# A decoder trunk whose first FFN multiplies tokens that are not yet normed, and loads x and its first weights in alternating halves

## The chip, the cores and the metric

The kernel runs on one core of a Trainium2 chip. The metric is the device time of one execution in microseconds; runs are told by their median. The engines of the core are TensorE (PE; its weight loads are shown as PEld), VectorE (DVE), ScalarE (ACT), GpSimd (POOL) and SyncE (SP), which issues most transfers.

## The reference, cut to what matters

Two layers of a hybrid decoder trunk work on 256 tokens of width 1024 in float32. The change lies in the first FFN of the first layer alone.

```python
def rms_norm(x, w):
    x32 = x.astype(jnp.float32)
    y = x32 * lax.rsqrt(jnp.mean(x32 * x32, axis=-1, keepdims=True) + EPS)
    return (y * w.astype(jnp.float32)).astype(x.dtype)

def swiglu(h, w_gate, w_up, w_down):
    return (jax.nn.silu(h @ w_gate) * (h @ w_up)) @ w_down

for l in range(DEPTH):                                   # DEPTH = 2
    x = x + 0.5 * swiglu(rms_norm(x, ffn1_norm[l]), ffn1_w_gate[l], ffn1_w_up[l], ffn1_w_down[l])
    x = x + hybrid_mixer(rms_norm(x, mix_norm[l]), ...)  # two head groups, HGRN2 and FoX
    x = x + memory_cross_attention(rms_norm(x, cross_norm[l]), rms_norm(mem, mem_norm[l]), ...)
    x = x + 0.5 * swiglu(rms_norm(x, ffn2_norm[l]), ffn2_w_gate[l], ffn2_w_up[l], ffn2_w_down[l])
return rms_norm(x, final_norm)
```

The width of an FFN (D_FF) is 2816. The norm of a token is a gain per feature times one number per token, the mean square to the power -1/2. The text calls this number the token's power.

## The kernel before, in words

**Products in three parts.** Every float32 operand is split in a high part in a reduced format (the cast writes it) and a low part (the operand minus its high part). A product is three TensorE instructions: high by high, high by low, low by high (`mm3`, L439 to L441). ScalarE makes the high parts (`whi` of weights, `xfh` of tokens), VectorE the low ones (`wlo`, `xfl`). For the first FFN of the first layer the gain per feature is multiplied into the weights while they are split (`split_k`, L147 and L148): it stands on the partitions of the weight tiles, in the column `g0`, which TensorE makes from a loaded row by a transpose (L229) and VectorE copies (L230).

**Weights.** All weights are one list of pieces of at most 1 MB (`plan`), four row blocks of 128 rows by 512 columns for the gate and the up matrices. `fetch` issues the loads on SP's queue into three buffers (`rawp`), `split` makes the two parts in seven buffers of two row blocks each (`wp`). A piece is fetched two pieces ahead of the one that is split and split one ahead of the one that is used. `split_block` splits one row block of a piece.

**Tokens.** x is resident as `xs`, two token blocks of 128 partitions by 1024 features. For the products, 128x128 squares are transposed on TensorE into a PSUM tile of four (`pt`), and `put_split` makes the two parts from it (ScalarE, then VectorE, L366 and L367).

**An FFN.** The 2816 columns are taken in five chunks of 512 and one of 256. The first chunk keeps tokens on the output's partitions: gate and up products of 512 columns with the tokens as stationary operand. For the others (`wstat`) weights are stationary, the 256 tokens are the columns, and a PSUM bank holds two column blocks of 128 features; `use_g` and `use_u` evict it: Silu on ScalarE (L697), multiplication on VectorE (L706), and a split. The down product `rows_to_residual` goes over all 22 row blocks, and its result times 0.5 is added to `xs` on VectorE (L628), after which the next norm begins.

**The beginning.** The first FFN's first gate block is written out by hand in `first_chunk`. Within an `in_order` block each engine keeps the order of the text; elsewhere the framework places an instruction in its engine's queue by a simulated time and by priority. Before that, `warm_up` issues transposes of the identity into a bank that nobody reads. `norm(t)` takes the squares of half 0 on ScalarE (L488) and of half 1 on VectorE (L489), sums them (L340) and lets GpSimd raise the sum to the power -1/2 (L341); `scaled` multiplies a half of x by it on VectorE (L494); `turn` transposes four squares (L501); `put` splits them. The first token block's products with weight blocks 0 to 3 come first, then 12 more warm-up transposes, then the second token block's norm and transposes, and the rest of the 16 products of the block (48 instructions).

**The rest.** The kernel's main line and side tasks (constants, the two head groups, the memory) are generators; `drive` picks by a clock of estimated times what is written next. The estimates (`yield` of a time) of the first chunk are the same in both kernels.

Of the kernel before, what the change touches and what calls it, by code (L numbers as in the profile page):

```python
# [8 lines left out]
F32 = mybir.dt.float32  # L9
# [4 lines left out]
ALU = mybir.AluOpType  # L14
# [31 lines left out]
def hymba_kernel(  # L46
# [82 lines left out]
    def fetch(i):  # L129
        while len(raws) <= min(i, len(plan) - 1):  # L130
            src, nk, cw, _ = plan[len(raws)]
            r = rawp.tile([P, 4 * 520], F32, name=nm("raw"), tag="raw")
            rv = r[:, :nk * cw].rearrange("p (k c) -> p k c", k=nk)
            n = (4, 2)[len(raws)] if len(raws) < 2 else 1
            for k0 in range(0, nk, nk // n):
                nc.sync.dma_start(out=rv[:, k0:k0 + nk // n, :], in_=src[:, k0:k0 + nk // n, :])
            raws.append(r)

    def split_k(i, sl, k, hi, lo):

# [66 lines left out]

    grow = cp.tile([8, P], F32, name="grow")
    nc.scalar.dma_start(out=grow, in_=ffn1_norm[0].rearrange("(k p) -> k p", p=P))
    for t in range(NT):  # L210
        for j in range(2):
            sl = slice(j * 512, (j + 1) * 512)
            nc.sync.dma_start(out=xs[:, t, sl], in_=x_d[0, t * P:(t + 1) * P, sl])
        fetch(t)


    ident = cp.tile([P, P], F32, name="ident")
# [3 lines left out]
    def warm_up(n):  # L221
        for i in range(n):
            nc.tensor.transpose(warm[:, (i % 4) * P:(i % 4 + 1) * P], ident, ident)
# [1 line left out]
    g0 = cp.tile([P, 8], F32, name="g0")  # L225
    g0t = smp("g0t")
    with in_order():
        warm_up(14)
        nc.tensor.transpose(g0t[:, 0:8], grow, ident[0:8, 0:8])  # L229
        nc.vector.tensor_copy(out=g0, in_=g0t[:, 0:8])  # L230
        gcols["first"] = g0
        warm_up(12)
    neghalf = cp.tile([P, 4], F32, name="neghalf")
    nc.vector.memset(neghalf, -0.5)

# [242 lines left out]

    def first_chunk(f, psa_, psb_):

        psa_ += [acc(), acc()]
        rs = [small(1, "rs") for _ in range(NT)]
        hn = [s4([P, D], F32, "hn") for _ in range(NT)]

        def norm(t):
            ss = small(2, "ss")
            x = xs[:, t, :]
            nc.scalar.activation(hn[t][:, 0:512], half(x, 0), AF.Square, scale=1.0 / 32.0, accum_out=ss[:, 0:1])  # L488
            nc.vector.tensor_tensor_reduce(out=hn[t][:, 512:1024], in0=half(x, 1), in1=half(x, 1), scale=1.0 / 1024.0,  # L489
                                           scalar=0.0, op0=ALU.mult, op1=ALU.add, accum_out=ss[:, 1:2])  # L490
            inv_rms(ss, rs[t])

        def scaled(t, j):
            nc.vector.tensor_scalar(out=half(hn[t], j), in0=half(xs[:, t, :], j), scalar1=rs[t], scalar2=None,  # L494
                                    op0=ALU.mult)

        def turn(t, b):
            pt = smp("pt")
            for j in range(4):
                kt = 4 * b + j  # L500
                nc.tensor.transpose(pt[:, j * P:(j + 1) * P], hn[t][:, kt * P:(kt + 1) * P], ident)  # L501
            return pt

        def put(pt, t, b):
            sl = slice(t * P, (t + 1) * P)
            put_split(f.h[b][:, :, sl], f.l[b][:, :, sl], pt.rearrange("p (k t) -> p k t", k=4))

        with in_order():
            norm(0)
            for j in range(2):  # L510
                scaled(0, j)
            p0 = [turn(0, b) for b in range(2)]
            pa = split_block(0, 0)
            put(p0[0], 0, 0)
            for kt in range(4):
                if kt:
                    pa += split_block(0, kt)
                xmm(psa_, f, kt, 0, pa[kt], 512)
            warm_up(12)
            put(p0[1], 0, 1)  # L520
            norm(1)
            pa += split_block(1, 0)
            for j in range(2):
                scaled(1, j)
            p1 = [turn(1, b) for b in range(2)]
            pa += split_block(1, 1)
            for b in range(2):
                put(p1[b], 1, b)
            for kt in (4, 5):
                xmm(psa_, f, kt, 0, pa[kt], 512)  # L530
            for kt in range(6):
                xmm(psa_, f, kt, 1, pa[kt], 512)
            for kt in (6, 7):
                pa += split_block(1, kt - 4)
                for t in range(NT):
                    xmm(psa_, f, kt, t, pa[kt], 512)
            taken[0] = 2
        yield 16 * T512
        yield from xstat(f, 512, psb_)

    def wstat(f, use, cw=512):

# [69 lines left out]
    def rows_to_residual(act, n, scale, tail, nxt, need=None):  # L612
        ps = [[[(acc(), 0, 512)] for _ in range(2)] for _ in range(NT)]
        if nxt.last:
            ps[1][1] = [(ps[1][1][0][0], 0, 256), (smp(), 256, 256)]
        head = n - tail

        def one(i, t, h, pc, pieces_):
            hi, lo = act(i, t)
            for a, c, w in pieces_:  # L620
                sl = slice(h * 512 + c, h * 512 + c + w)
                mm3(a[:, 0:w], hi, lo, pc[0][:, sl], pc[1][:, sl], i == 0, i == n - 1)

        def resid(t, h, piece):
            a, c, w = piece
            sl = xs[:, t, h * 512 + c:h * 512 + c + w]
            with tc.high_priority(offset=HP):
                nc.vector.scalar_tensor_tensor(out=sl, in0=a[:, 0:w], scalar=scale, in1=sl, op0=ALU.mult, op1=ALU.add)  # L628

        for i in range(0, head, 2):  # L630
            pc = take()
            for j in range(2):
                if need is not None:
                    yield need(i + j)
                for t in range(NT):
                    for h in range(2):
                        one(i + j, t, h, pc[j], ps[t][h])
                yield 4 * T512
        pcs = []
        for i in range(head, n, 2):  # L640
            pcs += take()
        for t in range(NT):
            for h in range(2):
                for piece in ps[t][h]:
                    for i in range(head, n):
                        if need is not None:
                            yield need(i)
                        one(i, t, h, pcs[i - head], [piece])
                        yield T512 * piece[2] / 512
                    resid(t, h, piece)  # L650
            nxt.start(t)


    def ffn(cur, nxt_w, last=False, first=False):
# [4 lines left out]
        def h_task(c, hs, cw):  # L659
# [25 lines left out]
        for ci, (c0, cw) in enumerate(FCH):  # L685
            g, u = [], []
            if ci == 0:
                if first:
                    yield from first_chunk(f, g, u)
                else:  # L690
                    yield from xstat_first(f, cur.ev, g, u)
                mult(ci, silu(g, cw), u, cw)
            else:
                s_ = s4([P, NT, 512], F32, "sil")

                def use_g(b, ps):
                    nc.scalar.activation(s_[:, b], ps, AF.Silu)  # L697

                yield from wstat(f, use_g, cw)
                hi = s4([P, 4, S], F32R, "hth")  # L700
                lo = s4([P, 4, S], F32R, "htl")
                hts[ci] = (hi, lo)

                def use_u(b, ps):
                    h = s_[:, b]
                    nc.vector.tensor_tensor(out=h, in0=h, in1=ps, op=ALU.mult)  # L706
# [237 lines left out]
    def mixer(cur, l, consts, nxt_w):  # L944
# [74 lines left out]
        def act(kt, t):  # L1019
            return oT.hi(kt, t), oT.lo(kt, t)  # L1020

        yield from rows_to_residual(act, KT, 1.0, TAIL, nxt, lambda kt: ev_h if kt < 4 else ev_p[kt - 4])
        return nxt, kc, vc, mf

    def memory_task(mf, ev):
# [32 lines left out]
    def cross(cur, kc, vc, mf, nxt_w):  # L1058
# [56 lines left out]
        def act(kt, t):  # L1115
            return oT.hi(kt, t), oT.lo(kt, t)

        yield from rows_to_residual(act, KT, 1.0, TAIL, nxt, lambda kt: evs[kt // 2])
        return nxt


# [45 lines left out]
```

## Time and profile before

| | |
|---|---|
| median of 3 runs | 1242.22 us (1242.09 to 1242.61) |
| the profiled execution | 1242.66 us, its span 1240.8 us |
| TensorE busy | 1227.8 us, 99% of the span |
| VectorE busy | 767.1 us, 62% |
| ScalarE busy | 653.6 us, 53% |
| loads | 219.72 MB, mean 177 GB/s |

The profile is one execution. Its page gives busy times by engine, the span in 40 slices, the chain of work that ended last, and groups of instructions by line. L439 is line 439 of the kernel; `acc<-xfh,whi` names the output tile and the input tiles. The span's start is 0 in all times of the order of instructions. The mean granted clock of TensorE was 0.999 of full speed. TensorE's instructions are pipelined: the duration of one is longer than the distance between the starts of two.

### The profile page before, as it was taken

The numbers are of one execution on the slowest core, as the hardware profiler recorded it, in microseconds if no ns is written. First come the engines' busy times: TensorE is split into PE (matmuls) and PEld (weight loads), VectorE is DVE, ScalarE is ACT, GpSimd is POOL, SyncE is SP. The second block draws the span as 40 slices with busy tenths as digits, with TensorE's granted clock in tenths as the row PEclk, the third lists the DMA queues.
The fourth block names the chain that finished last, engine by engine and source line by source line (L and its number), as shares of the span: only waits on it lengthen the run. The fifth ranks groups of instructions, "written<-read, shape, count | busy, mean of one in ns | idle before, by whom it ended". The sixth has DMA issues, their size and how long they took to land.

```text
span 1240.8 us, 21619 instructions
## 1 busy us (share of the span) xinstructions
PE 1227.8 (99%) x9074; PEld 1122.9 (90%) x9074; DVE 767.1 (62%) x1180; ACT 653.6 (53%) x1022; POOL 36.9 (3%) x52
## 2 busy tenths in 40 slices
PE   9999999999999999999999999999999999999997
PEld 7999888999989889998889998889998898999986
DVE  7756546588866674464474554475887766545643
ACT  7555535568854454353354454366786555444532
POOL 0000000011000000000000000000010000000000
PEclk9999999999999999999999999999999999999999
DMA  8555654643544374565474556465444533555640
GB/s 320 170 191 171 237 191 152 221 135 139 170 153 170 102 254 141 199 206 202 136 255 137 204 181 220 142 216 193 144 147 170 187 131 109 190 184 170 238 170 35
DMA packets 100258, 219.72 MB, mean 177 GB/s; under 512 B 4128, under 2 KB 16704, under 8 KB 100160
## 3 DMA queue, kind: packets, MB, share of 16 engines
q1 hardware_dynamic: 100000, 218.07, 51.7%
q8 instruction: 71, 1.16, 0.4%
q10 hardware_dynamic: 160, 0.27, 0.1%
q14 instruction: 27, 0.22, 0.1%
HBM read 217.28 MB, written 1.05 MB: 176 GB/s over the span
## 4 chain that ended last, share of the span: by engine, by line
PE 93%; DVE 3%; ACT 1%; POOL 1%; issue 1%; DMA 0%; POOLq 0%; SPq 0%; DVEq 0%; ACTq 0%
PE acc L439 29%; PE acc L440 29%; PE acc L441 29%; PE pt L360 1%; DVE wlo L144 1%; PE al L739 1%; DVE wlo L148 1%; ACT whi L147 0%; POOL rs L341 0%; POOL hrs L808 0%; PE cpo L440 0%; DVE pp L867 0%; PE cs L440 0%; PE cs L439 0%; PE cs L441 0%
## 5 line engine op out<-in xcount | busy, mean ns | idle before, releaser
L144 DVE TENSOR_TENSOR wlo<-raw,whi 128x1024 fp32r<-128x1024 f32 (+1 forms) x324 | 389.1, 1223 | 275.4 <-ACT whi L143 274.4
L143 ACT CAST whi<-raw 128x1024 fp32r<-128x1024 f32 (+1 forms) x324 | 330.4, 1048 | 276.1 <-PE acc L441 137.1
L439 PE MATMUL acc<-xfh,whi 128*128 128x256 f32 x1536 | 432.7, 282 | 0.0
L440 PE MATMUL acc<-xfl,whi 128*128 128x256 f32 x1536 | 431.6, 281 | 0.2
L441 PE MATMUL acc<-xfh,wlo 128*128 128x256 f32 x1536 | 430.1, 280 | 0.0
L440 PEld LDWEIGHTS acc<-xfl,whi 128*128 128x128 f32 x1536 | 290.3, 189 | 0.9 <-DVE xfl L367 0.7
L439 PEld LDWEIGHTS acc<-xfh,whi 128*128 128x128 f32 x1536 | 289.0, 188 | 0.8
L441 PEld LDWEIGHTS acc<-xfh,wlo 128*128 128x128 f32 x1536 | 289.7, 189 | 0.0
L439 PE MATMUL acc<-whi,hth 128*128 128x512 f32 (+1 forms) x352 | 136.4, 388 | 0.0
L440 PE MATMUL acc<-wlo,hth 128*128 128x512 f32 (+1 forms) x352 | 136.3, 387 | 0.0
L441 PE MATMUL acc<-whi,htl 128*128 128x512 f32 (+1 forms) x352 | 135.8, 386 | 0.0
L439 PE MATMUL acc<-whi,xfh 128*128 128x512 f32 (+1 forms) x256 | 94.8, 370 | 0.6 <-ACT xfh L366 0.6
L440 PE MATMUL acc<-wlo,xfh 128*128 128x512 f32 (+1 forms) x256 | 94.0, 367 | 0.0
L441 PE MATMUL acc<-whi,xfl 128*128 128x512 f32 (+1 forms) x256 | 93.6, 366 | 0.1
L441 PEld LDWEIGHTS acc<-whi,htl 128*128 128x128 f32 x352 | 66.2, 188 | 14.5
L439 PEld LDWEIGHTS acc<-whi,hth 128*128 128x128 f32 x352 | 66.1, 188 | 14.4
L440 PEld LDWEIGHTS acc<-wlo,hth 128*128 128x128 f32 x352 | 66.1, 188 | 14.0
L148 DVE SCALAR_TENSOR_TENSOR wlo<-raw,g,whi 128x512 fp32r<-128x512 f32 (+1 forms) x96 | 61.9, 703 | 26.0 <-PE acc L441 18.5
L147 ACT ACTIVATE whi<-raw,g 128x512 fp32r<-128x512 f32 (+1 forms) x96 | 58.2, 678 | 24.8 <-PE acc L440 18.0
L439 PEld LDWEIGHTS acc<-whi,xfh 128*128 128x128 f32 x256 | 48.1, 188 | 9.2 <-ACT xfh L366 0.8
L441 PEld LDWEIGHTS acc<-whi,xfl 128*128 128x128 f32 x256 | 48.1, 188 | 8.9 <-DVE xfl L367 0.4
L440 PEld LDWEIGHTS acc<-wlo,xfh 128*128 128x128 f32 x256 | 48.2, 188 | 8.6 <-DVE wlo L148 0.4
(257 smaller groups left out, 1503.5 us busy)
## 6 DMA issues: line engine op xcount, KB each, us to landing
raw<-in_ffn_w_down_dram SPq DMA_DIRECT2D x44, 1024.0 KB, 4.9
raw<-in_ffn_w_up_dram SPq DMA_DIRECT2D x40, 1024.0 KB, 5.2
raw<-in_ffn_w_gate_dram SPq DMA_DIRECT2D x38, 1024.0 KB, 5.1
raw<-in_w_in_dram SPq DMA_DIRECT2D x24, 1024.0 KB, 5.2
raw<-in_cross_wk_dram SPq DMA_DIRECT2D x8, 1024.0 KB, 5.0
raw<-in_cross_wv_dram SPq DMA_DIRECT2D x8, 1024.0 KB, 5.1
raw<-in_w_out_dram SPq DMA_DIRECT2D x8, 1024.0 KB, 4.8
raw<-in_cross_wq_dram SPq DMA_DIRECT2D x8, 1024.0 KB, 5.1
```

Source lines behind the costliest of these rows:

```text
L143: nc.scalar.copy(out=hi, in_=sl)
L144: nc.vector.tensor_tensor(out=lo, in0=sl, in1=hi.bitcast(F32), op=ALU.subtract)
L147: nc.scalar.mul(hi, sl, g)
L148: nc.vector.scalar_tensor_tensor(out=lo, in0=sl, scalar=g, in1=hi.bitcast(F32), op0=ALU.mult, op1=ALU.subtract)
L360: nc.tensor.transpose(pt[:, j * P:(j + 1) * P], hn[:, kt * P:(kt + 1) * P], ident)
L439: nc.tensor.matmul(ps, lhsT=lh, rhs=rh, start=start, stop=False)
L440: nc.tensor.matmul(ps, lhsT=lh, rhs=rl, start=False, stop=False)
L441: nc.tensor.matmul(ps, lhsT=ll, rhs=rh, start=False, stop=stop)
L739: nc.tensor.matmul(ps[s0:s0 + hb, c0:c0 + hb], lhsT=k[:, h, a:a + hb], rhs=rhs[:, h, a + step:a + step + hb], start=True, stop=True)
```

## The change

Six edits belong together.

1. The first FFN of the first layer transposes x as loaded (`xs`) and not x times its power. With r the powers and z the products of gained but unscaled tokens, the gate is silu(r * z_gate), the up product stays z_up, and r is applied to the down product's sum together with 0.5: the residual adds (0.5 * r) * (sum over features of silu(r * z_gate) * z_up * w_down).
2. The squares are taken later, between the splits of weight blocks 5, 6 and 7; the powers follow after them.
3. In the first chunk tokens lie on partitions, so Silu takes the power as its scale per partition. In the other chunks tokens are columns: a row of the powers, repeated on all partitions, is made by filling a 128x128 tile with the power of each partition and transposing it, for each token block. `use_g` multiplies the PSUM bank by this row on VectorE into SBUF, and Silu reads that.
4. The order of `first_chunk` is new: the first four squares of both token blocks are transposed first, each weight block is used for both token blocks, and the other halves of x are transposed before weight block 3's products.
5. The loads: half 0 of token block 0, weight block 0, half 0 of token block 1, weight blocks 1 to 3, the two other halves of x, and then weight blocks 4 to 7, now in four transfers and not two.
6. The warm-up transposes are 9 and 6, where they were 14, 12 and 12.

The diff; the callers of `rows_to_residual` that don't belong to the first FFN pass a list of the constant they passed before.

```diff
@@ fetch
-            n = (4, 2)[len(raws)] if len(raws) < 2 else 1
+            n = 4 if len(raws) < 2 else 1
             for k0 in range(0, nk, nk // n):
                 nc.sync.dma_start(out=rv[:, k0:k0 + nk // n, :], in_=src[:, k0:k0 + nk // n, :])
+                for t, j in ({0: [(1, 0)], 3: [(0, 1), (1, 1)]}.get(k0, []) if not raws else []):
+                    load_x(t, j)
             raws.append(r)
+
+    def load_x(t, j):
+        sl = slice(j * 512, (j + 1) * 512)
+        nc.sync.dma_start(out=xs[:, t, sl], in_=x_d[0, t * P:(t + 1) * P, sl])
@@ the beginning
-    for t in range(NT):
-        for j in range(2):
-            sl = slice(j * 512, (j + 1) * 512)
-            nc.sync.dma_start(out=xs[:, t, sl], in_=x_d[0, t * P:(t + 1) * P, sl])
-        fetch(t)
+    load_x(0, 0)
+    for i in range(2):
+        fetch(i)
...
-        warm_up(14)
+        warm_up(9)
         nc.tensor.transpose(g0t[:, 0:8], grow, ident[0:8, 0:8])
         nc.vector.tensor_copy(out=g0, in_=g0t[:, 0:8])
         gcols["first"] = g0
-        warm_up(12)
@@ first_chunk: norm(t) and scaled(t, j) are gone; turn(t, b) reads xs; put(pt, t, b) is as it was
+        rs = [small(1, "rs0", bufs=2) for _ in range(NT)]
+        sq = [s4([P, D], F32, "sq") for _ in range(NT)]
+        sums = [small(2, "ss") for _ in range(NT)]
+        pa = []
...
+        def part(kt, t, which):
+            x = (f.hi, f.hi, f.lo)[which](kt, t)
+            w = (pa[kt][0], pa[kt][1], pa[kt][0])[which]
+            nc.tensor.matmul(psa_[t], lhsT=x, rhs=w, start=kt == 0 and which == 0, stop=kt == KT - 1 and which == 1)
+
+        def block(kt, order=(0, 2, 1)):
+            first = order[:2] if order[1] == 2 else order[:1]
+            for t in range(NT):
+                for w in first:
+                    part(kt, t, w)
+            for w in order[len(first):]:
+                for t in range(NT):
+                    part(kt, t, w)
+
+        def squares(t):
+            x = xs[:, t, :]
+            nc.scalar.activation(sq[t][:, 0:512], half(x, 0), AF.Square, scale=1.0 / 32.0, accum_out=sums[t][:, 0:1])
+            nc.vector.tensor_tensor_reduce(out=sq[t][:, 512:1024], in0=half(x, 1), in1=half(x, 1), scale=1.0 / 1024.0,
+                                           scalar=0.0, op0=ALU.mult, op1=ALU.add, accum_out=sums[t][:, 1:2])
+
         with in_order():
+            p0 = turn(0, 0)
+            warm_up(6)
+            put(p0, 0, 0)
+            pa += split_block(0, 0)
+            part(0, 0, 0)
+            part(0, 0, 2)
+            p1 = turn(1, 0)
+            put(p1, 1, 0)
+            part(0, 0, 1)
+            for w in (0, 2, 1):
+                part(0, 1, w)
+            for kt in (1, 2):
+                pa += split_block(0, kt)
+                block(kt)
+            pa += split_block(0, 3)
+            p = [turn(t, 1) for t in range(NT)]
+            block(3)
+            pa += split_block(1, 0)
+            for t in range(NT):
+                put(p[t], t, 1)
+            block(4, (0, 1, 2))
+            for kt in (5, 6, 7):
+                pa += split_block(1, kt - 4)
+                if kt < 7:
+                    squares(kt - 5)
+                block(kt)
             taken[0] = 2
+            for t in range(NT):
+                inv_rms(sums[t], rs[t])
         yield 16 * T512
         yield from xstat(f, 512, psb_)
+        rb = sq[0].rearrange("p (j t) -> p j t", j=8)
+        pt = smp("rt")
+        for t in range(NT):
+            nc.vector.tensor_scalar(out=rb[:, t, :], in0=ident, scalar1=0.0, scalar2=rs[t], op0=ALU.mult, op1=ALU.add)
+            nc.tensor.transpose(pt[:, t * P:(t + 1) * P], rb[:, t, :], ident)
+        row = sm.tile([P, S], F32, name=nm("L"), tag="L", bufs=1)
+        nc.vector.tensor_copy(out=row, in_=pt[:, 0:S])
+        hrs = [small(1, "hrs0", bufs=2) for _ in range(NT)]
+        for t in range(NT):
+            nc.vector.tensor_scalar(out=hrs[t], in0=rs[t], scalar1=0.5, scalar2=None, op0=ALU.mult)
+        return rs, hrs, row
@@ resid
-                nc.vector.scalar_tensor_tensor(out=sl, in0=a[:, 0:w], scalar=scale, in1=sl, op0=ALU.mult, op1=ALU.add)
+                nc.vector.scalar_tensor_tensor(out=sl, in0=a[:, 0:w], scalar=scale[t], in1=sl, op0=ALU.mult, op1=ALU.add)
@@ ffn
+        rs, scale, row = [1.0] * NT, [0.5] * NT, None
...
-                nc.scalar.activation(s_[:, t, :cw], g[t][:, :cw], AF.Silu)
+                nc.scalar.activation(s_[:, t, :cw], g[t][:, :cw], AF.Silu, scale=rs[t])
...
-                    yield from first_chunk(f, g, u)
+                    rs, scale, row = yield from first_chunk(f, g, u)
...
                 def use_g(b, ps):
+                    if row is not None:
+                        nc.vector.tensor_tensor(out=s_[:, b].rearrange("p (k t) -> p k t", k=2),
+                                                in0=ps.rearrange("p (k t) -> p k t", k=2),
+                                                in1=row.unsqueeze(1).to_broadcast([P, 2, S]), op=ALU.mult)
+                        ps = s_[:, b]
                     nc.scalar.activation(s_[:, b], ps, AF.Silu)
...
-        yield from rows_to_residual(act, FT, 0.5, TAIL, nxt, lambda kt: evs[kt // 4])
+        yield from rows_to_residual(act, FT, scale, TAIL, nxt, lambda kt: evs[kt // 4])
```

More of the change, by code (lines that the diff above doesn't have):

```diff
@@ L481, in first_chunk @@
         psa_ += [acc(), acc()]
[L482 to L495, printed above, removed]
+        rs = [small(1, "rs0", bufs=2) for _ in range(NT)]
+        sq = [s4([P, D], F32, "sq") for _ in range(NT)]
+        sums = [small(2, "ss") for _ in range(NT)]
+        pa = []
         def turn(t, b):
@@ L500, in turn @@
                 kt = 4 * b + j
-                nc.tensor.transpose(pt[:, j * P:(j + 1) * P], hn[t][:, kt * P:(kt + 1) * P], ident)
+                nc.tensor.transpose(pt[:, j * P:(j + 1) * P], xs[:, t, kt * P:(kt + 1) * P], ident)
             return pt
@@ L506, in put @@
             put_split(f.h[b][:, :, sl], f.l[b][:, :, sl], pt.rearrange("p (k t) -> p k t", k=4))
-        with in_order():
[L509 to L521, printed above, removed]
-            pa += split_block(1, 0)
[L523 to L533, printed above, removed]
+        def part(kt, t, which):
+            x = (f.hi, f.hi, f.lo)[which](kt, t)
+            w = (pa[kt][0], pa[kt][1], pa[kt][0])[which]
+            nc.tensor.matmul(psa_[t], lhsT=x, rhs=w, start=kt == 0 and which == 0, stop=kt == KT - 1 and which == 1)
@@ L1020, in act @@
             return oT.hi(kt, t), oT.lo(kt, t)
-        yield from rows_to_residual(act, KT, 1.0, TAIL, nxt, lambda kt: ev_h if kt < 4 else ev_p[kt - 4])
+        yield from rows_to_residual(act, KT, [1.0] * NT, TAIL, nxt, lambda kt: ev_h if kt < 4 else ev_p[kt - 4])
         return nxt, kc, vc, mf
@@ L1116, in act @@
             return oT.hi(kt, t), oT.lo(kt, t)
-        yield from rows_to_residual(act, KT, 1.0, TAIL, nxt, lambda kt: evs[kt // 2])
+        yield from rows_to_residual(act, KT, [1.0] * NT, TAIL, nxt, lambda kt: evs[kt // 2])
         return nxt
```

2 lines of the change are left out of this document (removed).

## The prediction

> **What bounds the kernel now.** I read the page's totals first, then the chain of waits, then the order of time of the opening 36 us.
>
> ```profile
> span 1240.8 us, 21619 instructions
> ...
> PE 1227.8 (99%) x9074; PEld 1122.9 (90%) x9074; DVE 767.1 (62%) x1180; ACT 653.6 (53%) x1022; POOL 36.9 (3%) x52
> ...
> PE 93%; DVE 3%; ACT 1%; POOL 1%; issue 1%; DMA 0%; POOLq 0%; SPq 0%; DVEq 0%; ACTq 0%
> ```
>
> TensorE sets the end: 93% of the chain. A microsecond taken out ahead of its stream shortens the run by a microsecond, if nothing that feeds the stream was only just in time. The profiled execution took 1242.66 us (span 1240.8), the median of the runs is 1242.22, so the sum below, made on the span, is taken off the median.
>
> The chain of waits in order of time (start, length, what) shows what precedes the stream:
>
> ```profile
> 0.74 0.39 SPq L213
> 1.18 3.60 DMA xs<-in_x_dram
> 4.81 0.69 DVE hn L489
> 5.87 0.56 POOL rs L341
> ...
> 7.45 0.72 ACT whi L147
> ...
> 8.64 1.85 ACT whi L147 x3
> ...
> 13.09 1.05 POOL rs L341
> 14.17 0.50 DVE hn L494
> 14.71 1.09 PE pt L501 x8
> 15.80 0.23 PE acc L439
> ```
>
> Both halves of a token's row must land (4.78), be squared, summed, raised to a power on GpSimd and multiplied in, before anything is transposed; the second token block does this again, from 10.9 to 14.7. Only at 15.8 does the chain become TensorE's own. TensorE's rows, and two stretches (TensorE's busy time is the second number):
>
> ```profile
> 1.36 3.25 PE L223 MATMUL warm<-ident 128*128 128x128 f32 x14 [1.36 <-POOL ident masks.py:199]
> 4.74 2.44 PE L223 MATMUL warm<-ident 128*128 128x128 f32 x12
> 7.02 1.07 PE L501 MATMUL pt<-ident,hn 128*128 128x128 f32 x8
> 12.22 1.47 PE L223 MATMUL warm<-ident 128*128 128x128 f32 x12
> 15.56 0.48 PE L439 MATMUL acc<-whi,xfh 128*128 128x512 f32 x1
> 23.96 0.40 PE L439 MATMUL acc<-whi,xfh 128*128 128x512 f32 x1
> 35.14 0.28 PE L439 MATMUL acc<-xfh,whi 128*128 128x256 f32 x1
> ```
> ```profile
> 15.56:23.96 8.40, 8.40 (x40) 6.86 (x39) 8.09 (x13) 8.37 (x14) 0.00 (x0) 1.00 0.97 343
> 35.14:160.00 124.86, 124.86 (x968) 120.61 (x967) 78.21 (x157) 67.65 (x105) 0.00 (x0) 1.00 0.56 188
> ```
>
> From 15.56 on it is full. Between there and 35.14 lie 84 products of 512 columns (36 left of the first gate block's 48, and 48 of its up block), so one takes (35.14 - 15.56)/84 = 0.233 us. The 36 end at 23.96, the mark I compare with: when does the first gate block's last product end afterwards?
>
> **The change, part by part.** The normalizing leaves the front: transposes read x as it lands. The rows for the pieces that remain:
>
> ```profile
> 3.62 0.63 ACT L488 ACTIVATE hn<-xs 128x512 f32<-128x512 f32 x1 [0.98 <-DMA xs<-in_x_dram]
> ...
> 7.25 0.16 DVE L230 COPY g<-g0t 128x8 f32<-128x8 f32 x1
> ...
> 8.07 0.56 ACT L366 CAST xfh<-pt 128x512 fp32r<-128x512 f32 x1
> ...
> 8.54 1.95 ACT L147 ACTIVATE whi<-raw,g 128x512 fp32r<-128x512 f32 x3
> ...
> 12.05 0.68 DVE L489 CUSTOM_DVE_ANT_0 hn<-xs 128x512 f32<-128x512 f32 x1
> ...
> 15.40 1.07 ACT L366 CAST xfh<-pt 128x512 fp32r<-128x512 f32 x2 [2.60 <-PE pt L501]
> ...
> 16.02 1.29 DVE L367 TENSOR_TENSOR xfl<-pt,xfh 128x512 fp32r<-128x512 f32 x2 [0.29 <-ACT xfh L366]
> ...
> 16.37 6.25 ACT L147 ACTIVATE whi<-raw,g 128x512 fp32r<-128x512 f32 x10
> ...
> 17.23 6.71 DVE L148 SCALAR_TENSOR_TENSOR wlo<-raw,g,whi 128x512 fp32r<-128x512 f32 x10
> ```
>
> *Loads.* SP's issues and, for the tiles of the first 16 us, time from issue to landing (weights, then x):
>
> ```profile
> 1.66 1.85 SPq L136 DMA_DIRECT2D raw<-in_ffn_w_gate_dram  x4
> ...
> 4.49 1.34 SPq L136 DMA_DIRECT2D raw<-in_ffn_w_gate_dram  x2
> ```
> ```profile
> DMA to landing us min/median/max: 4.2/6.6/9.3
> ```
> ```profile
> DMA to landing us min/median/max: 2.9/3.6/5.4
> ```
>
> Pieces of 256 KB land in the order issued: the first of x at 0.74 + 2.9 = 3.6 (ScalarE starts on it at 3.62), the second piece issued at 4.8, the third, now the first weight block, at 1.66 + 4.2 = 5.9, the eighth about 4.0 + 5.4 = 9.4. Twelve pieces of one size in another order carry the same 3 MB, so I give the n-th piece the n-th landing: weight block 0 at 4.8, the second token block's first half at 5.9, weight blocks 1 to 3 by 8.3, the rest of x by 9.4. The four last pieces were two of 512 KB, landing from 4.49 + 6.6 = 11.1 at the earliest; in quarters they land at about 10.3 to 12.5. SP has two issues more, of about 0.45 us each, ahead of the up weights; the transfers queued then are longer than that, so I cost them at nothing.
>
> *Start of the products.* Nine fillers end at 1.36 + 9 x 0.23 = 3.4, the gains' column is turned, x turns at 3.66. TensorE paces here at 2.44/12 = 0.20 a transpose: the fourth starts at 4.27 and ScalarE casts 0.35 after that start (second token block: 15.40 against 14.71 + 3 x 0.12), at 4.65. Its next instruction follows 0.47 later (8.07, 8.54), so weight block 0 has its high half from 5.1 to 5.85 and the first product starts at 5.9, against 8.69 before. The low half of x starts 0.62 after the cast (15.40, 16.02) and ends at 5.95, so the second product can follow. Then four transposes of the second token block (piece landed at 5.9), a cast at 7.05, its low half from 7.67 to 8.35, three products around it. From 8.87 on TensorE waits for nothing: 42 products x 0.233 + 8 transposes of 0.12 = 10.7, ending at **19.6**. If TensorE still keeps the slow pace, 2.44/1.47 = 1.66 times as long per step, until the second token block is turned, the cast comes 0.6 later and the end is **20.2**. I take 19.9: a gain of 23.96 - 19.9 = 4.1 us.
>
> *Feeding it.* A weight block costs ScalarE 0.63 and VectorE 0.67 (6.25/10, 6.71/10); four casts 0.56 and low halves 0.65; the two halves of the squares 0.63 + 0.19 and 0.68 + 0.08, now between weight blocks 5 to 7. Laid out in the order written, VectorE finishes the last low block at 17.8; TensorE wants it at 19.1. The smallest margin is 0.6 us, at block 4, where the low half of x is ready at 14.3 and wanted at 14.9.
>
> *Powers at the gates.* Row sums go to GpSimd at about 18, the power is there by 19.3 (1.05 us) and the first gate's Silu needs it at 20, with three blocks of products to spare before its PSUM bank is wanted. Silu with a pointer scale isn't in the trace; between the plain Silu below (0.59) and L147's scaled activation (0.65): 0 to +0.06, hidden. The row of powers for the other chunks costs VectorE two 128x128 fills, a copy and two tiny products (about 1 us, while it waits for weights at 24 to 25) and TensorE two transposes, 0.25 us on the path. Each of the nine later gate evictions gets a VectorE multiplication from PSUM with a broadcast operand; nearest rows (out, count, min/median/max ns):
>
> ```profile
> L697 ACT ACTIVATE sil<-acc x9: 574/589/600, 41.9 to 133.7; 128x512 f32<-128x512 f32 x9
> L706 DVE TENSOR_TENSOR sil<-sil,acc x9: 680/682/689, 53.5 to 139.2; 128x512 f32<-128x512 f32 x9
> ```
>
> So 9 x 0.68 = 6.1 us of VectorE, with 0.68 more latency before each Silu. The Silu's result is used one stage (11 us) later and there are four accumulator banks, so the cover is wide: VectorE is busy 78.2 of 124.9 us there. Cost 0; without that cover 6.1. The residual's scale becomes a pointer: four instructions, 0 to 0.05 each, counted as 0.
>
> *What is late next.* The loads are nearly saturated (0.97 of the engines' time up to 23.96), so the weights behind must be there 4 us sooner. Gate chunk 1's splits before:
>
> ```profile
> 24.70 2.57 ACT L147 ACTIVATE whi<-raw,g 128x512 fp32r<-128x512 f32 x4 [0.17 <-DMA raw<-in_ffn_w_gate_dram]
> ...
> 28.39 2.74 DVE L148 SCALAR_TENSOR_TENSOR wlo<-raw,g,whi 128x512 fp32r<-128x512 f32 x4 [0.19 <-ACT whi L147]
> ```
>
> The eight blocks are done at 31.1 on the old timetable. TensorE would come to them at 35.14 - 4.1 = 31.1 and need the fifth only 12 products of 0.12 later, at 32.5. Even unmoved they are in time, by little; I expect them half a microsecond earlier, since the raw buffers come free earlier. Sum: -4.1 + 0.25 = -3.8 us, **1238.4**; own range 1237.4 to 1239.6.
>
> **The fillers and a rule.** TensorE's transposes took 0.20 each up to 7 us and 0.12 after it (2.44/12, 1.47/12), with nothing but transposes before the change of pace. The Trainium skill, "TensorE: Matmul & The Clock Gate", Part 4: PE-mode transpose, says that transposes don't bring the array to its full clock; the trace differs, so the sum keeps the measured pace; by that rule the array would wake only some 3.4 us (the page's window, Part 1) into the products, an estimate of 0.5 to 1.5 us less gain.
>
> **Rivals.**
> 1. *The array wakes late.* 38 fillers become 15. Before, the pace rose after 5.7 us of filler; counted anew from the first product that is 11.6. Products from 8.9 to 11.6 at 1.66 times the time lose 2.7 x 0.4 = 1.1, and the second token block's 0.6 is paid in full (0.3 of it is in the sum): 1238.4 + 1.4 = 1239.8. For: fewer fillers, gaps around 7 to 8.5. Against: TensorE is busy almost without gap from 1.36 to 6.9.
> 2. *The gains' copy stands late on VectorE*, as at 7.25 before, three microseconds after its transpose. Behind the first low half it would come at 6.1 instead of 3.9, and weight block 0 waits 1.0 us: 1239.4. Against: little else is queued there now.
> 3. *The weights take it back.* If gate chunk 1 lands later, because x and weights in quarters cost the queue more, TensorE stalls at 31 to 33 and the gain shrinks to 1 us or nothing: 1241.3 to 1242.2. For: the margin of about 1.5 us on a saturated queue. Against: the same bytes in the same time.
> 4. *Slower: the gate multiplications reach TensorE.* Each would delay the weight splits queued behind it on VectorE. From 3.8/9 = 0.42 us exposed per gate the gain is gone; all exposed gives 1238.4 + 6.1 = 1244.5. For: VectorE carries the splits that TensorE eats. Against: 46.6 us idle there, and the splits run up to seven buffers ahead.
>
> **How the numbers follow.** Likeliest 0.52; rival 1 0.12, rival 2 0.11, rival 3 0.17, rival 4 0.08. A difference under 0.2%, 2.5 us, is about what a measurement of this kernel can't tell from none; the bound is 1239.74. Above it lie rivals 3 and most of 4, half of rival 1: faster 0.52 + 0.11 + 0.06 and a little of 4, 0.70; within 0.2% 0.17 + 0.06 = 0.23; slower 0.07. The range 1237.0 to 1241.4 leaves out most of rival 4, part of rival 3 and the tails.
>
> **What will show it.** First product near 5.9 and the first gate block's end between 19.6 and 20.2; no wait of TensorE for VectorE or a load between 9 and 35; 128-column steps of 0.12 us from about 7; VectorE some 5 us busier before 140 with TensorE full. It is wrong if TensorE waits at 31 to 33, if the first weight block waits for the gains' column, or if gaps appear at the gate ends.

## The result, and the profile after

The changed kernel takes 1235.99 us (median of four runs, 1235.51 to 1236.02) against 1242.15 for the kernel before on the same chip: a ratio of 0.995 [0.9932, 0.9967], a gain of 6.2 us where 3.8 were forecast. It is faster, as predicted, but the time lies outside the range. The profiled execution took 1236.02 us with a span of 1234.2.

The page of the kernel after, its busy times and its chain of waits by engine:

```profile
span 1234.2 us, 21594 instructions
PE 1222.1 (99%) x9053; PEld 1118.8 (91%) x9053; DVE 770.2 (62%) x1190; ACT 653.7 (53%) x1022; POOL 36.6 (3%) x52
...
PE 93%; DVE 4%; ACT 1%; POOL 1%; issue 1%; DMA 0%; POOLq 0%; ACTq 0%
```

TensorE still bounds the kernel; it is busy 5.7 us less (1227.8 before). The opening, as the chain that ended last (start, length, engine, operation):

```profile
0.74 3.23 DMA xs<-in_x_dram
4.01 1.12 PE pt L495 x4
5.13 1.28 PE warm L227 x6
6.43 1.09 PE acc L505 x2
7.52 0.45 PE pt L495 x4
7.99 0.59 ACT xfh L369
8.61 0.70 DVE xfl L370
9.35 3.50 PE acc L505 x14
12.85 0.87 PE pt L495 x8
13.73 6.99 PE acc L505 x30
```

The norm is gone from the head of the chain: the landing of the first piece of x leads straight to transposes and to a product at 6.43. Behind the first product, the second token block's cast and subtraction (7.99, 8.61) cost TensorE the only two gaps of the opening; from 9.35 it runs on without one. TensorE's timeline shows the pace and the first use of an up weight, that is, the end of the first gate block:

```profile
9.92 0.39 PE L505 MATMUL acc<-whi,xfh 128*128 128x512 f32 x1
10.15 0.39 PE L505 MATMUL acc<-whi,xfl 128*128 128x512 f32 x1
...
20.55 0.39 PE L442 MATMUL acc<-whi,xfh 128*128 128x512 f32 x1
...
193.61 0.93 PE L363 MATMUL pt<-ident,hn 128*128 128x128 f32 x7
...
802.78 0.82 PE L363 MATMUL pt<-ident,hn 128*128 128x128 f32 x6
...
1168.58 0.28 PE L442 MATMUL smp<-whi,hth 128*128 128x256 f32 x1
```

The gate block ends at 20.55, 3.41 us sooner than the 23.96 of before. The last three rows are marks: the transposes of two later norms (eight each; the view's window leaves out the last) and the first products of a late stage. The same marks in TensorE's timeline of the kernel before:

```profile
197.45 0.82 PE L360 MATMUL pt<-ident,hn 128*128 128x128 f32 x6
...
808.87 0.93 PE L360 MATMUL pt<-ident,hn 128*128 128x128 f32 x7
...
1175.03 0.28 PE L439 MATMUL smp<-whi,hth 128*128 128x256 f32 x1
```

The lead is 3.84 us at the first mark, 6.09 at the second, 6.45 at the third. It grows by some 2.6 us between 194 and 1169, in stages that the diff does not touch and in which TensorE is full in both kernels. So the gain has two parts: about 3.4 in the opening, and about 3 gathered along the rest of the run, not at one place but not evenly either (2.25 between the first two marks, 0.36 between the last two). The second part was not in the prediction.

### The profile page after: what moved, and what is told of

Same layout as the page of the kernel before. It is cut to its first block, busy times and chain, and to the rows that moved or that the text cites. A ratio compares the mean times of both kernels' runs of the same rounds, so it can differ in the third digit from the quotient of the medians.

```text
span 1234.2 us, 21594 instructions
## 1 busy us (share of the span) xinstructions
PE 1222.1 (99%) x9053; PEld 1118.8 (91%) x9053; DVE 770.2 (62%) x1190; ACT 653.7 (53%) x1022; POOL 36.6 (3%) x52
## 2 busy tenths in 40 slices
DMA packets 100290, 219.73 MB, mean 178 GB/s; under 512 B 4160, under 2 KB 16736, under 8 KB 100192
## 4 chain that ended last, share of the span: by engine, by line
PE 93%; DVE 4%; ACT 1%; POOL 1%; issue 1%; DMA 0%; POOLq 0%; ACTq 0%
PE acc L442 29%; PE acc L443 29%; PE acc L444 28%; DVE wlo L150 1%; PE pt L363 1%; PE acc L505 1%; PE al L771 1%; DVE wlo L154 1%; DVE xfl L370 0%; POOL rs L344 0%; POOL hrs L840 0%; DVE pp L899 0%; PE cpo L443 0%; PE cs L442 0%; PE cs L444 0%
## 5 line engine op out<-in xcount | busy, mean ns | idle before, releaser
L442 PE MATMUL acc<-whi,xfh 128*128 128x512 f32 (+1 forms) x240 | 87.8, 366 | 0.0
L443 PE MATMUL acc<-wlo,xfh 128*128 128x512 f32 (+1 forms) x240 | 87.3, 364 | 0.0
L444 PE MATMUL acc<-whi,xfl 128*128 128x512 f32 (+1 forms) x240 | 87.1, 363 | 0.0
L154 DVE SCALAR_TENSOR_TENSOR wlo<-raw,g,whi 128x512 fp32r<-128x512 f32 (+1 forms) x96 | 62.0, 702 | 19.9 <-PE acc L444 11.4
L369 ACT CAST hth<-sil 128x512 fp32r<-128x512 f32 x36 | 22.3, 619 | 56.8 <-DVE sil L738 56.8
L444 PEld LDWEIGHTS acc<-whi,xfl 128*128 128x128 f32 x240 | 45.1, 188 | 7.6
L442 PEld LDWEIGHTS acc<-whi,xfh 128*128 128x128 f32 x240 | 45.1, 188 | 7.6
```

Of the source, the lines that this page charges most:

```text
L154: nc.vector.scalar_tensor_tensor(out=lo, in0=sl, scalar=g, in1=hi.bitcast(F32), op0=ALU.mult, op1=ALU.subtract)
L369: nc.scalar.copy(out=hi, in_=src)
L442: nc.tensor.matmul(ps, lhsT=lh, rhs=rh, start=start, stop=False)
L443: nc.tensor.matmul(ps, lhsT=lh, rhs=rl, start=False, stop=False)
L444: nc.tensor.matmul(ps, lhsT=ll, rhs=rh, start=False, stop=stop)
```

## The experiments

**What grows.** From each trace I took the starts of consecutive TensorE products of one width into the accumulator tiles (`acc`) and averaged the distances (those under 1.4 times the median, which leaves gaps out). A product of 256 columns took 117.92 ns before and 117.66 after, one of 512 columns 232.65 and 231.82. The groups of three lines give 4608 of the first kind and some 1,800 of the second: 4608 x 0.26 ns + 1,800 x 0.83 ns = 2.7 us, about what the marks show.

**A difference that the diff doesn't write.** The seven buffers of split weights (a high and a low part each, 4160 bytes per partition) are handed out by the framework, which gives a new tile a buffer that its own estimate of times holds to be free. That the changed order of the first lap changed this choice is the likely reason, not a tested one. The order of the first lap then repeats, so the buffers form a ring. Numbering the places in SBUF (the on-chip memory that TensorE reads its operands from) from 0, the order was, in use:

```
before  high 0 6 5 4 3 2 1    low 0 6 5 4 3 1 2
after   high 0 6 5 4 1 2 3    low 0 6 5 4 1 2 3
```

Before, the last two pairs were crossed: the high part at place 2 went with the low part at place 1, and the reverse. Sorted by place, the three products of a 256-column block took 359.6 ns for the pair high 2, low 1, and 351.4 to 353.8 for the six others; after, all seven lie between 349.5 and 355.7. Theory P: the places alone make the part behind the opening. Rival Q: it comes from the change itself (gate multiplications, loads, other work on VectorE).

### Places exchanged, first attempt

Both kernels get a ring with fixed places, each kernel the other's:

```diff
-    wp = ctx.enter_context(tc.tile_pool(name="wp", bufs=N_W))
+    wp = ctx.enter_context(tc.tile_pool(name="wp", bufs=1))
+    RING_HI, RING_LO = [0,6,5,4,1,2,3], [0,6,5,4,1,2,3]   # in the kernel before
+    RING_HI, RING_LO = [0,6,5,4,3,2,1], [0,6,5,4,3,1,2]   # in the kernel after
+    def slots():
+        k = turn_[0] % N_W; turn_[0] += 1
+        return (wp.tile([P, SLOT], F32R, name=nm("whi"), tag=f"whi{RING_HI[k]}"),
+                wp.tile([P, SLOT], F32R, name=nm("wlo"), tag=f"wlo{RING_LO[k]}"))
-                hi = wp.tile([P, SLOT], F32R, name=nm("whi"), tag="whi")
-                lo = wp.tile([P, SLOT], F32R, name=nm("wlo"), tag="wlo")
+                hi, lo = slots()
```

The kernel before with the places of after:

> The kernel before, instruction for instruction, with the seven buffer pairs of split weights taken in the order of places that the changed kernel has (the high parts in 0, 6, 5, 4, 1, 2, 3, the low parts in 0, 6, 5, 4, 1, 2, 3 of theirs) in place of its own (0, 6, 5, 4, 3, 2, 1 and 0, 6, 5, 4, 3, 1, 2). Theory (the places of the weights set TensorE's pace, and that is the half of the gain that the opening does not explain): about 3 us faster than before, 1239, with 256-column products at 117.6 ns and not 117.9. Rival (the pace goes with something else: the new program, other tiles, the chip): no difference, 1242.

The kernel after with the places of before:

> The changed kernel with the weights' buffers in the order of places of the kernel before; nothing else differs. Theory (places set the pace): about 3 us slower than the changed kernel, 1239, with products as before (117.9 ns) and the opening's 3.3 us kept. Rival: 1236 as the changed kernel.

Neither came as expected: 1244.97 us (ratio to before 1.0023 [1.0014, 1.0032]) and 1245.4 (1.0025 [1.0014, 1.0035]). Separate buffers gave the framework another order of ScalarE's and VectorE's work in the opening: some splits of up weights moved ahead and waited for their loads. ScalarE's waits in the first of the two, 9 to 40 us:

```profile
ACT whi L161 <- DMA raw<-in_ffn_w_up_dram: 4.0, 1, 4.0
```

So the totals decide nothing. The paces do speak: 117.65 and 231.80 ns in the kernel before with the new places, 117.95 and 232.68 in the kernel after with the old ones. Both values had changed sides.

### Powers at the gates left out

This kernel leaves the tokens' powers out of the nine later gates. It has fixed places too (those of after), and the same disturbed opening.

```diff
-                    if row is not None:
+                    if False:
```

> The changed kernel without the nine multiplications of the gates by the row of powers: the five later chunks of the first FFN take Silu of unscaled products, and that part of the computation is left out. The order of the weights' places is kept as in the changed kernel. Theory (VectorE does them beside TensorE): 1236, within 0.5 us. Rival (they reach TensorE): up to 6 us faster, 1230.

1241.89 us, 0.9998 [0.9988, 1.0007]. The total is spoilt by the opening again, but the marks bracket the gates. TensorE's timeline in this kernel:

```profile
38.01 0.38 PE L571 MATMUL rt<-ident,sq 128*128 128x128 f32 x2
...
200.00 0.93 PE L376 MATMUL pt<-ident,hn 128*128 128x128 f32 x7
```

and in the kernel after, the same first mark, and its multiplications (count, ns):

```profile
31.62 0.38 PE L558 MATMUL rt<-ident,sq 128*128 128x128 f32 x2
```
```profile
L725 DVE TENSOR_TENSOR sil<-acc,L x9: 675/685/692, 39.2 to 130.0; 128x512 f32<-128x512 f32 x9
```

The distance is 6.39 us at the first mark and 6.39 (200.00 - 193.61) at the second. Between them lie the nine multiplications, 6.2 us of VectorE in the one kernel and none in the other: their cost to TensorE is nothing. What lost the 6.4 us is in the windows of this kernel (length, busy us of PE, PEld, DVE, ACT, POOL; granted clock; DMA share; GB/s):

```profile
9.00:17.60 8.60, 5.96 (x29) 4.51 (x28) 4.42 (x7) 4.26 (x8) 0.00 (x0) 1.00 1.03 388
17.60:24.40 6.80, 5.79 (x14) 4.44 (x15) 6.80 (x16) 6.80 (x14) 0.82 (x1) 0.50 0.77 276
```

TensorE waited once for 3.4 us of the first window; for the 6.8 us behind it the array ran at a granted clock of 0.50. The gap and the slow stretch both count.

### The first attempt at the load order

Fixed places, and x loaded ahead of the weights in the old order:

```diff
-                for t, j in ({0: [(1, 0)], 3: [(0, 1), (1, 1)]}.get(k0, []) if not raws else []):
-                    load_x(t, j)
...
-    load_x(0, 0)
-    for i in range(2):
-        fetch(i)
+    for t in range(NT):
+        for j in range(2):
+            load_x(t, j)
+        fetch(t)
```

> The changed kernel with the loads in the order of before: token block 0 whole, weight blocks 0 to 3, token block 1 whole, weight blocks 4 to 7. Theory (the second token block's first half is now the late one: it lands at about 8.9 in place of 5.9 and TensorE waits with its transposes queued): 1.5 to 2 us slower than the changed kernel, 1237.5 to 1238. Rival (deferring the norm is all of it, the order of the loads is hidden): 1236.

1240.01 us, 0.9983 [0.9974, 0.9992]; the opening carries the same disturbance, so the number belongs to both edits.

### Places exchanged, with every engine's order kept

One line more, at the end of the block in which the first chunk's order is written out, pins the splits to where the framework had put them. The order of each engine's instructions is then that of the kernel it was made from, and the places are the only difference. The experiments from here on have this line.

```diff
+            split(3)
```

The kernel before with the places of after:

> The first kernel with the changed kernel's order of places of the split weights, and every engine's order of instructions now exactly that of the kernel before (in the earlier try some splits of the up weights had moved ahead in ScalarE's and VectorE's queues and stalled the opening by 3 to 4 us). Theory (places alone set TensorE's pace, worth 3.1 us): 1239.0, the offset to the kernel before growing evenly over the run by 0.25 us per 100 us, the opening untouched. Rival (the pace belongs to the changed program): 1242.1.

The kernel after with the places of before, and the kernel after with its own places as a control:

> The changed kernel with the first kernel's order of places of the split weights, every engine's order of instructions unchanged. Theory: the opening's 3.3 us stay and the pace's 3.1 go: 1239.1. Rival: 1236.

> The changed kernel with its order of places written out by hand, the same addresses and the same order of instructions on every engine: 1236.0 by every theory; it is what the others of this chip are measured against.

| kernel | places | us (range) | ratio to before | 256 col., ns | 512 col., ns |
|---|---|---|---|---|---|
| before | before's | 1242.15 | 1 | 117.92 | 232.65 |
| before | after's | 1239.37 (1238.92–1239.86) | 0.9978 [0.9968, 0.9987] | 117.67 | 231.86 |
| after | before's | 1239.34 (1238.73–1241.52) | 0.9979 [0.9969, 0.9988] | 117.93 | 232.69 |
| after | after's | 1236.33 (1235.92–1236.55) | 0.9952 [0.9935, 0.9968] | 117.67 | 231.86 |

Theory P holds from both sides: the places take 2.8 us from the kernel before and give 3.0 back to the kernel after; the rest of the change takes 2.8 or 3.0 whichever places it meets. Rival Q falls. The marks of the kernel before with the places of after:

```profile
196.63 0.93 PE L373 MATMUL pt<-ident,hn 128*128 128x128 f32 x7
...
806.60 0.93 PE L373 MATMUL pt<-ident,hn 128*128 128x128 f32 x7
...
1172.01 0.28 PE L452 MATMUL smp<-whi,hth 128*128 128x256 f32 x1
```

Its lead on the kernel before is 0.82, 2.27 and 3.02 us: it grows with time, as a pace does and a single stall does not.

### The load order alone

The edit of the first attempt, now with every other order kept:

> The changed kernel with the loads in the order of before (token block 0 whole, weight blocks 0 to 3, token block 1 whole, the rest), all other orders and places kept. Theory (the second token block's half lands at 8.9 and not at 5.9 and TensorE waits for it): 1.5 to 2.5 us slower than the changed kernel, 1238. Rival (the order of the loads is hidden): 1236. If the wait also lets the array fall back to half its pace: 1239 or more, with half-pace stretches in the clock.

1240.18 us (1239.02 to 1241.23), 0.9983 [0.9973, 0.9992]: 3.85 more than the control. TensorE's timeline:

```profile
6.90 0.79 PE L517 MATMUL acc<-whi,xfh 128*128 128x512 f32 x1 [0.63 <-ACT whi L165]
7.49 0.63 PE L517 MATMUL acc<-whi,xfl 128*128 128x512 f32 x1
8.80 1.12 PE L507 MATMUL pt<-ident,xs 128*128 128x128 f32 x4 [0.68 <-DMA xs<-in_x_dram]
...
12.33 0.63 PE L517 MATMUL acc<-whi,xfh 128*128 128x512 f32 x1
12.76 0.63 PE L517 MATMUL acc<-whi,xfl 128*128 128x512 f32 x1
...
17.19 1.03 PE L507 MATMUL pt<-ident,xs 128*128 128x128 f32 x8
...
18.52 0.40 PE L517 MATMUL acc<-whi,xfh 128*128 128x512 f32 x1
18.76 0.40 PE L517 MATMUL acc<-whi,xfl 128*128 128x512 f32 x1
```

Behind a whole token block the first weight block comes late too, and TensorE waits 0.63 us for its high part; then it waits 0.68 us for the second token block. That is the small part: the products behind stand 0.43 us apart until 16.9, and only then 0.24. The eight transposes, at 12.69 in the kernel after, come at 17.19, 4.5 us late. The next two experiments tell how far the late pace may be put down to these waits. With the kernel before at 1242.15 and the places worth 3.0, the change without its load order would, by this sum, have come out 1 us slower than the kernel before (1240.18 + 3.0 = 1243.2).

### Six fillers out

The fillers (warm-up transposes) between the first transposes and the first product are taken out:

```diff
-            warm_up(6)
```

> The changed kernel without the six warm-up transposes between the first four squares of x and the first product. Theory (they only fill the gap from 4.9 to 6.4 and keep the array from losing its pace): if the array still wakes near 7, 1236; if it now wakes one step of 3.4 us later, as with x loaded first, it is half-paced from 7 to 10.4 or 17 and the run is 1 to 4 us longer, 1237 to 1240. I take 1238. Rival (fillers are of no use): 1236.

1238.83 us (1237.49 to 1240.09), 0.9974 [0.9964, 0.9984]: 2.5 more than the control. TensorE's timeline:

```profile
6.34 0.79 PE L518 MATMUL acc<-whi,xfh 128*128 128x512 f32 x1 [1.29 <-ACT whi L167]
...
11.26 0.63 PE L518 MATMUL acc<-whi,xfl 128*128 128x512 f32 x1
11.69 0.63 PE L518 MATMUL acc<-whi,xfh 128*128 128x512 f32 x1
```

The first product is no later (6.34 against 6.43), but TensorE has nothing to do for 1.29 us ahead of it, and full pace comes at 14.5; in the control's trace it comes at 7.4. The fillers are worth something: each of the eight executions took longer than the longest of the control, by 0.9 to 3.5 us. That the gap made the pace late is not shown. In two traces with every filler, and no gap between them and the first product, full pace came as late: at 13.8 in the first attempt's kernel after with the old places, and at 13.6 with the aligned places of the next experiment. In six others with these fillers and this order of loads it came by 7.4.

### Other places

Three rings on the changed kernel: pairs matched and rising; places of 4224 bytes behind a pad of 64, so that all operands start on multiples of 128 bytes; pairs matched, but falling as in before.

```diff
+    RING_HI, RING_LO = [0,1,2,3,4,5,6], [0,1,2,3,4,5,6]   # rising
-SLOT = 1040                                               # aligned, ring of after
+SLOT = 1056
+    cp.tile([P, 16], F32, name="pad")
+    RING_HI, RING_LO = [0,6,5,4,3,2,1], [0,6,5,4,3,2,1]   # falling
```

> The changed kernel with the weights' places taken in rising order, 0 to 6, high and low alike. If the pace depends on which place follows which (groups of three products with the pairs reached by a rising step took 349.5 to 353.9 ns, by a falling step 352.9 to 355.7): 1 to 3 us faster, 1234. If only the two mismatched pairs of the kernel before matter (high part in place 2 with low part in 1, and the other way round): 1236.

> The changed kernel with every place of the split weights 4224 bytes long in place of 4160, and all tiles moved by 64 bytes, so that every weight and token operand starts on a multiple of 128 bytes; orders kept. If the pace depends on the operands' position within 128 bytes (weights on a multiple of 128: 117.6 ns, 64 off: 118.0): 1 to 4 us faster, 1233 to 1235. If only the order of places matters: 1236. Slower is open as well, since I don't know what in the addresses counts.

> The changed kernel with the weights' places in falling order all through (0, 6, 5, 4, 3, 2, 1) and high and low parts always in places of the same number; the kernel before had this order too, but with the low parts of the last two exchanged. Theory M (the exchanged pairs are what slowed the kernel before: its group of three with the high part in place 2 took 359.6 ns, all others 351 to 354): 1236.3, as the changed kernel. Theory D (falling steps are slow and rising ones quick): 1239, as the changed kernel with the old places.

Rising: 1235.64 us (1235.44 to 1238.36), 0.9957 [0.9943, 0.9971]; the fastest median, but 0.35 from the 1235.99 of the changed kernel is no win that these runs can tell, and most of its 0.7 against the control lies in the opening. In its trace full pace came at 5.3 us, two earlier than in the control's. Falling: 1236.79 (1236.49 to 1237.02), 0.9956 [0.994, 0.9973]; it differs from the places of before only in that the two crossed pairs are matched, and that alone is worth 2.55 of the 3.0 us (1239.34 - 1236.79). The matching is not all: its products of 512 columns have the pace of the kernel after (231.80 ns), those of 256 columns (117.84) lie between those of the control and those with the places of before. Aligned: 1241.29 (1240.67 to 1243.54), 0.9997 [0.9988, 1.0007], 5.0 more than the control, the opposite of what a rule of alignment would give. Its marks, and first its opening, with all fillers and without a gap:

```profile
4.79 1.49 PE L241 MATMUL warm<-ident 128*128 128x128 f32 x6
6.29 0.79 PE L519 MATMUL acc<-whi,xfh 128*128 128x512 f32 x1
...
11.64 0.63 PE L519 MATMUL acc<-whi,xfh 128*128 128x512 f32 x1
12.07 0.63 PE L519 MATMUL acc<-whi,xfl 128*128 128x512 f32 x1
...
196.61 0.93 PE L377 MATMUL pt<-ident,hn 128*128 128x128 f32 x7
...
808.51 0.93 PE L377 MATMUL pt<-ident,hn 128*128 128x128 f32 x7
```

and those of the control:

```profile
193.63 0.93 PE L376 MATMUL pt<-ident,hn 128*128 128x128 f32 x7
...
802.91 0.82 PE L376 MATMUL pt<-ident,hn 128*128 128x128 f32 x6
```

2.98 and 5.60 us: in this execution the opening lost some 2 (products 0.43 us apart, full pace only at 13.6), and the rest is pace, 118.69 ns a product of 256 columns. The profiled execution took 1243.21 us, 1.9 more than the median; of the median's 5.0 us the pace makes 4608 x 1.02 ns = 4.7. Products of 512 columns are no slower there (231.76 ns). That addresses set the pace is shown; why one pair of addresses is slow stays open.

## Why the prediction was right in direction and wrong in size

**The step that failed** is the sum "-4.1 + 0.25 = -3.8": it has no term for the stages behind the opening. A product there was held at what it took before ("12 products of 0.12"), and so the change of buffer places, which the prediction did not name, was costed at nothing. It was worth 3.0 us of the 6.2. With the old places the changed kernel takes 1239.34, inside the prediction's own range of 1237.4 to 1239.6. That half of the gain was luck: none of the six edits aims at the places.

**Opening.** Forecast 4.1, measured 3.41 at the end of the gate block (20.55 against 19.9; the bounds of 19.6 and 20.2 were missed too). The first product came at 6.43 instead of 5.9. TensorE's first transposes and ScalarE's first cast in the kernel after:

```profile
4.01 1.12 PE L495 MATMUL pt<-ident,xs 128*128 128x128 f32 x4 [0.27 <-DMA xs<-in_x_dram]
```
```profile
5.17 0.59 ACT L369 CAST xfh<-pt 128x512 fp32r<-128x512 f32 x1 [2.53 <-PE pt L495]
5.65 0.72 ACT L153 ACTIVATE whi<-raw,g 128x512 fp32r<-128x512 f32 x1
```

The first piece landed at 3.97 (0.74 + 3.23, forecast 3.6) and the cast came at 5.17 (forecast 4.65): half a microsecond. The slow pace, which lasted to 7.2 ("about 7") and so over the first product and the start of the second, made another half: the second cast came at 7.99 (forecast 7.05), and the 42 products begin at 9.92, not at 8.87. The 19.9 held 0.3 of this slow pace and none of the late landing. The mechanism was right and these terms mis-sized. The two transposes of the row of powers put off the next product by 0.14 us (31.62 to 31.76), where 0.25 was forecast.

**Rival 1, the array wakes late**, didn't happen in the traced execution of the change (full pace at 7.2). It is real: in the kernel with x loaded first and in the one without six fillers full pace came at 16.9 and 14.5, and their medians are 3.85 and 2.5 us above the control, waits included, more than the forecast's 1.4. But it came at 13.6 and 13.8 in two kernels with all fillers and no gap, so neither "fewer fillers" nor the gaps alone decide it; what does stays open.

**Rival 2, the gains' copy**, was wrong. VectorE copies the column at once:

```profile
3.78 0.17 DVE L234 COPY g<-g0t 128x8 f32<-128x8 f32 x1 [2.33 <-PE g0t L233]
```

**Rival 3, the weights take it back**, was wrong. The waits of TensorE that the view lists up to 36 us:

```profile
PE warm L227 <- POOL ident masks.py:199: 1.4, 1, 1.4
PE acc L505 <- ACT xfh L369: 0.4, 1, 0.4
PE pt L495 <- DMA xs<-in_x_dram: 0.3, 1, 0.3
PE acc L505 <- DVE xfl L370: 0.2, 1, 0.2
```

None is for a weight. **Rival 4, the gate multiplications reach TensorE**, was wrong: nine of 0.685 us (forecast 0.68), hidden as argued, shown by leaving them out. VectorE was busy 6.2 us more up to 140 us (100.56 against 94.32; forecast some 5).

**The rule weighed.** By the Trainium skill ("TensorE: Matmul & The Clock Gate", Part 4: PE-mode transpose) transposes don't bring the array to its full clock. The traces disagree again: with nothing but transposes on TensorE until then, the pace rose at 6.65 us in the kernel before (first product 8.69) and at 5.26 with the rising places (first product 6.31). In the kernel before, the transposes stood 0.21 us apart up to that point and 0.11 behind it; the prediction's 0.20 "up to 7 us" averaged over the rise.

## What to carry to other kernels

Where TensorE is full, compare the mean distance of its products in untouched stages before reading a gain of some tenths of a per cent as the work of an edit; an edit in the first lap of a ring of buffers can reorder the ring for the whole run, as it likely did here. When an experiment changes buffers, keep every engine's order fixed in the same edit, or the order is what is measured. Ahead of the first products a filler that costs nothing is worth trying: six of them were worth 2.5 us here. It doesn't assure an early full pace, so look at the pace in the trace, and at more than one execution, before a late rise is put down to an edit.

## What the runs showed of the hardware

*Operand addresses set TensorE's pace.* With the same instructions in the same order, a product of 256 columns took 117.51 to 118.69 ns depending on where in SBUF the operands lay, 1% between the ends. The one layout on multiples of 128 bytes, in which all tiles had moved by 64 bytes, was the slowest for 256 columns and not for 512 (231.76 ns, against 231.80 to 232.69 in the others).

*When full pace comes is not fixed.* By the first entry of each trace's clock record, where the distances of TensorE's starts change too, the same fillers and first products reached it by 7.4 us in six traces and at 13.6 and 13.8 in two; the kernel before reached it at 6.65, and at 4.91 with the new places and its order kept.

*A gap is dear.* After the waits of the disturbed openings the array ran at half clock for 3.41 us (18.55 to 21.96, the kernel before with new places, after a wait of 4.4 us; 20.65 to 24.06, the kernel after with old places, after one of 1.6) and 6.83 us (17.61 to 24.44, the kernel without gate powers, after one of 3.4). The Trainium skill ("TensorE: Matmul & The Clock Gate", Part 1: The HAM clock gate) gives a free-running window of 3413 ns; one and two of them fit.

*The clock row doesn't show the start.* In the kernel with x loaded first the products of 512 columns stand 0.43 us apart up to 16.9 us, yet the windows give a granted clock of 1.00 there:

```profile
9.00:17.00 8.00, 7.75 (x20) 5.61 (x20) 3.36 (x5) 3.04 (x5) 0.00 (x0) 1.00 1.05 384
```

Ahead of the first rise only the distance of the products tells the pace.
